# Rows of tokens for the last residual: transposing transfers of 16-bit halves in place of TensorE transposes

## The chip, the cores and the metric

The kernel runs on one core of a Trainium2 chip. The metric is the device time of one execution in microseconds (us); the median of a few runs is compared. A profiled execution gives a trace: TensorE's matmuls (PE) and weight loads (PEld), VectorE (DVE), ScalarE (ACT), GpSimd (POOL), and SyncE (SP), which here only issues DMA transfers.

## The reference

One block of a streaming encoder over 512 tokens of 1024 features, in float32. What matters here:

```
x = x + 0.5 * swiglu(rms_norm(x, ffn1_norm), ffn1_w1, ffn1_w3, ffn1_w2)
h = rms_norm(x, mix_norm); p = h @ w_in
y_a = rwkv7_mixer(...) @ rwkv_proj ; y_b = fox_mixer(...) @ fox_proj
x = x + (gate_a * y_a + gate_b * y_b) @ w_out
x = x + 0.5 * swiglu(rms_norm(x, ffn2_norm), ffn2_w1, ffn2_w3, ffn2_w2)
out = rms_norm(x, final_norm)
swiglu(h, w1, w3, w2) = (silu(h @ w1) * (h @ w3)) @ w2
```

The x after `w_out` is used twice: as the input of the second FFN, and once more as the last residual, to which the FFN's result is added.

## The kernel before, in words

**Layout.** Through the mixer x is kept with features on the partitions: eight tiles `xT[m]` of 128 features x 512 tokens (2 KB a partition), the tiles `xS` by the end. The second FFN's last product gives the other layout, tokens on the partitions. So its residual has to be there by token: a DRAM tensor `osave` of 4 blocks x 128 tokens x 1024 features holds it, and is read back near the end of the kernel.

**Products.** Every float32 product is three matmuls (`mm3`, L173-176): the weights and the data are each split into a high part, rounded to the matmul's format by ACT, and the rest, by DVE (`split_w`, L163-168; tiles `whi`, `wlo`, two of each; the raw weights have three buffers, `raw`). A product of 128 output features over 1024 inputs is 24 matmuls of 128x512.

**The w_out product** (L2061-2069) runs over m = 0 to 7. For each it loads and splits weights, runs 24 matmuls into the bank `pw`, adds half of that to `xT[m]` on DVE, and calls `nrm2.add(m)`: DVE splits the scaled tile into `xh`, `xl`, ACT squares it, and POOL adds the square into `acc` (DVE does the last addition). The engines' order in this loop is the scheduler's, except that the products follow each other.

**The memory around it.** Everything of the mixer that is not needed longer lies in the pool `sp`, closed at the end of the loop by `sctx.close()`. `gslot` names halves of its tiles `G` (512 floats a partition each), free during the w_out product. The second FFN's buffers come from the pool `hp`, which takes over the same memory: the weights' buffers `ca`, `cd`, `cb`, `cc`, `u` and the tiles `seven.lo`, `seven.hi` (`rl`, `rh` in the profile).

**The start of the second FFN.** The raw weights of four products are requested on SP (`load_raw`), then `wide.begin()` requests ten loads of 512 KB into `cd`, `ca`, `cc`, `u`, `cb`, in this order and on SP. From `written(True)` on, the instructions of DVE, ACT and TensorE are issued in the order in which the program writes them (class `Queued`, L87-104; its instructions all have line L102 in the profile). POOL and SP stay with the scheduler. That order is: the first product `pa` (24 matmuls); the sum over squares (`ssum`, two matmuls) and its root (`rstd`, on ACT); then `tokens(m)` for eight m among the matmuls of the product `pb`, with `wide.normal` (DVE, scales the tile of x in place by gain and root) and `wide.weight(0, 0)` (splits the first half of `cd`: ACT's `sraw`, then DVE's) between; then the split of the fourth weights (`whi`, `wlo`) and the products `pa` and `pb` that follow.

`tokens(m)`, the function that the change replaces: four TensorE transposes of 128x128 into a bank `ot`, one ACT copy out of it into `o` (a free half of `seven.hi`, or a temporary), and one POOL store into `osave`.

Of the kernel before, what the change touches and what calls it, by code (L numbers as in the profile page):

```python
# [9 lines left out]
F32 = mybir.dt.float32  # L10
F32R = mybir.dt.float32r
BF16 = mybir.dt.bfloat16
AF = mybir.ActivationFunctionType
ALU = mybir.AluOpType
AX = mybir.AxisListType
# [3 lines left out]
P = 128  # L19
T = 512  # L20
D = 1024
KD = D // P
# [6 lines left out]
NB = T // P  # L29
# [52 lines left out]
def kernel(  # L82
# [6 lines left out]
    nc = tc.nc  # L89
# [16 lines left out]
    pool = nc.gpsimd  # L106
    dve, act, pe = [Queued(e, False) for e in (nc.vector, nc.scalar, nc.tensor)]
# [11 lines left out]
    pf = ctx.enter_context(tc.tile_pool(name="pf", bufs=3, space=PSUM))  # L119
    dp = ctx.enter_context(tc.tile_pool(name="dp", bufs=1, space=DRAM))  # L120

    def bank(name, pool_=None):
        pool_ = pool_ or pm
        return pool_.tile([P, T], F32, tag="b", name=name)

    def tmp(name, shape=(P, T), dt=F32, tag="t", **kw):
        return tp.tile(list(shape), dt, tag=tag, name=name, **kw)


    ident = cp.tile([P, P], F32, name="ident")  # L130
    make_identity(nc, ident)
    identb = cp.tile([P, P], BF16, name="identb")
    dve.tensor_copy(identb[:], ident[:])
# [15 lines left out]
    gmask = cp.tile([P, 2, C], F32, name="gmask")  # L149
    dmask = cp.tile([P, T], BF16, name="dmask")  # L150
    sel = cp.tile([P, 8], F32, name="sel")
# [18 lines left out]
    def load_w(aps, kt, n, eng=None):  # L170
        return split_w(load_raw(aps, kt, n), kt, n, eng)
# [6 lines left out]
    def ln_act(out, in_, **kw):  # L178
        pre = act.preload_act_table_set("natural_log_exp_and_others")
        tc.keep_in_program_order(pre)  # L180
        tc.keep_in_program_order(act.activation(out, in_, AF.Ln, **kw))

# [22 lines left out]
    def on(do, *a):  # L205
        return lambda: do(*a)

    class Plan:
# [4 lines left out]
        def op(s, engine, us, do, *deps, rank=0, takes=(), frees=(), later=0.0, kind="w"):  # L213
            s.ops.append(dict(engine=engine, do=do, deps=deps, takes=takes, frees=frees, done=False))
            return s.ops[-1]
# [20 lines left out]
    xT = [xQ[c // 4][:, c % 4] for c in range(KD)]  # L236
# [9 lines left out]
    class Norm:  # L246
# [7 lines left out]
        def scale(s, c, eng=None, src=None):  # L254
# [3 lines left out]
            if eng is act:  # L258
                high = act.activation(hi[:], src, AF.Copy, scale=g)
            else:  # L260
# [6 lines left out]
        def square(s, c, eng=None, src=None):  # L267
            src = xT[c][:] if src is None else src
            if s.n == 0:
                s.acc = xp.tile([P, T], F32, tag="acc", name="acc", bufs=2)  # L270
                act.activation(s.acc[:], src, AF.Square)
            else:
                sq = tmp("sq")
                act.activation(sq[:], src, AF.Square)
                if s.n < KD - 1:
# [26 lines left out]
    def pc(i):  # L302
        return par[:, i:i + 1]
# [12 lines left out]
    with tc.tile_pool(name="x0", bufs=1) as x0:  # L316
# [27 lines left out]
        def x_hi(c):  # L344
            nrm.hi[c] = pair("h", c)
            from_ = xps[c][:]
            if c % 2:
                qact.activation(nrm.hi[c][:], from_, AF.Copy, scale=pc(PAR_FFN1 + c))
            else:
# [24 lines left out]
        def square(c):  # L374
            if c == 0:
                nrm.acc = xp.tile([P, T], F32, tag="acc", name="acc", bufs=2)
                qact.activation(nrm.acc[:], xT[c][:], AF.Square)
            else:
# [666 lines left out]
    with tc.tile_pool(name="hp", bufs=1) as hp:  # L1045
        hp.tile([P, 96], F32, name="lead")
        wide = Wide(hp, Middle, nrm, ffn1_w1[0], ffn1_w3[0], ffn1_w2[0], xQ,
                    [x[0, b * P:(b + 1) * P, :] for b in range(NB)], C1)
        seven1, rows = wide.seven, []
# [26 lines left out]
        return [(0, W[:, c0:c0 + n])]  # L1076

    nrm2 = Norm(PAR_FFN2)
    with ExitStack() as mx:
        rp = mx.enter_context(tc.tile_pool(name="rp", bufs=1))  # L1080
        sctx = ExitStack()
# [100 lines left out]
        for o, c0, mu in ((spare[2], DA, 4), (spare[3], 0, 0)):  # L1182
            ps = bank("pk", pf)
# [3 lines left out]
        for p in range(NP):  # L1187
            za.append((zslots[2 * p], zslots[2 * p + 1]))
            for i, (w_, x_, par0, o) in enumerate(((uw, lw, PAR_W0, zslots[2 * p]), (ux, lx, PAR_A0, zslots[2 * p + 1]))):
                ps = bank("pz", (pr, pf)[i])  # L1190
# [181 lines left out]
        for t in range(C - 1):  # L1372
            n, m = t + 1, C - 1 - t
# [82 lines left out]
        for b in range(NB):  # L1456
            o = vtp.tile([P, T], F32, name=f"vt{b}", tag=f"vt{b}")
# [12 lines left out]
        rows = [Rows(p, n) for p in range(2) for n in range(2)]  # L1470
# [26 lines left out]
        for q in range(2):  # L1497
            o = (1 - q) * 64
# [11 lines left out]
        for q in range(2):  # L1510
            o = (1 - q) * 64
# [9 lines left out]
        for q in range(2):  # L1521
            pool.memset(Rs[0][half(q), :, q, :], 0.0)
            for i in range(RN):
                o = (1 - q) * 64
# [8 lines left out]
        o = op("ACT", 0.69, b1.log, summed, rank=SCAN, takes=["t"], frees=["pf"])  # L1533
        o = op("ACT", 0.63, b1.root, o, rank=SCAN)
# [110 lines left out]
        for c in range(NC):  # L1645
# [4 lines left out]
            if c % 4 == 3 and c < NC // 2:  # L1650
                o = op("SP", 0.4, on(fetch, nc.sync, c + 5, 4), e, later=4.0)
# [40 lines left out]
        def columns(name, at):  # L1692
            w, split_ = weights(at)

            def some(k):
                if k == 0:
                    w.ps = bank(name)
                mix.cols(w.ps[:], w.hi, w.lo, P, [], [k], k == 0, k == KD - 1)

            for k in range(KD):  # L1700
                fills.append(op("PE", 0.68, on(some, k), split_, *fills[-1:], rank=FILL,
                                takes=["pm"] * (k == 0), frees=["w"] * (k == KD - 1)))
            return w, fills[-1]
# [36 lines left out]
        for m in range(NP + 3, 2 * KD):  # L1740
            g = Held()
            w, o = columns("pgt", COL_GA + m * P)
# [11 lines left out]
            o = op("DVE", 0.61, result, o, rank=NEXT, takes=["gs"], frees=["pm"])  # L1754
            if m + 1 < 2 * KD:
                o = op("ACT", 0.55 if tanhs else 1.84, opened, o, *roots, rank=ROWS)
# [6 lines left out]
        sees, turned, exps, copies, yb = [], ([], []), [], [], []  # L1763
# [143 lines left out]
        o = []  # L1907
        for p in range(NP):
            o = op("ACT", 0.63, on(part_y, p), *outs[p], *sees, *o, rank=FILL)
            o = [op("DVE", 0.69, on(part_l, p), o, rank=FILL)]  # L1910
# [6 lines left out]
        def proj(m, wt, y, w=None):  # L1917
            wh, wl = w or proj_w(m, wt)
            ps = bank("ppj")
            for k in range(NP):  # L1920
                mm3(ps[:], wh[:, k, :], wl[:, k, :], y[k][0], y[k][1], k == 0, k == NP - 1)
            return ps


        def halves(tiles):
            return [t[:, i * 8:(i + 1) * 8].rearrange("p c a t -> p (c a t)") for t in tiles for i in range(2)]

        gslot = halves([g for gg in G for g in gg])
# [11 lines left out]
        ycs, sqs, pgs, pus, parts = [None] * NP, [None] * NP, [None] * NP, [None] * NP, {}  # L1940
# [70 lines left out]
        ps = proj(0, fox_proj, ybs, fws[0])  # L2011
        for m in range(KD):
# [11 lines left out]
            if m + 1 < KD:  # L2024
                ps = proj(m + 1, fox_proj, ybs, fws[m + 1])
# [29 lines left out]
        for m in range(KD):  # L2055
            g = slot[m]
            ps = proj(m, rwkv_proj, ya)
# [4 lines left out]
        for m in range(KD):  # L2062
            wh, wl = load_w([(0, w_out[0][:, m * P:(m + 1) * P])], KD, P)
            ps = bank("pw")
            with tc.issue_after(done.ins) if m else ExitStack():
                for k in range(KD):
                    done = mm3(ps[:], wh[:, k, :], wl[:, k, :], ms[k][0], ms[k][1], k == 0, k == KD - 1)
            dve.scalar_tensor_tensor(xT[m][:], ps[:], 0.5, xT[m][:], op0=ALU.mult, op1=ALU.add)
            nrm2.add(m)
        sctx.close()  # L2070


# [56 lines left out]
                nc.sync.dma_start(out[0, P:2 * P, low], o)  # L2129
                queue.dma_start(out[0, P:2 * P, high], o2)  # L2130

    osave = dp.tile([NB, P, D], F32, name="osave")
    with tc.tile_pool(name="hp", bufs=1) as hp:
        hp.tile([P, 96], F32, name="lead")
        wide = Wide(hp, Last, nrm2, ffn2_w1[0], ffn2_w3[0], ffn2_w2[0], xS, osave)

        def tokens(m):
            ps = bank("ot", pf)
            for b in range(NB):
                pe.transpose(ps[:, b * P:(b + 1) * P], xT[m][:, b * P:(b + 1) * P], ident[:])  # L2140
            o = wide.seven.hi[1][:, m] if m < 4 else tmp("on")[:]
            act.copy(o, ps[:])
            nc.gpsimd.dma_start(osave[:, :, m * P:(m + 1) * P].rearrange("b p c -> p b c"),
                                o.rearrange("p (b c) -> p b c", b=NB))

        raws = [load_raw([(0, w[:, j * P:(j + 1) * P])], KD, P) for j in range(2) for w in wide.w]
        wide.begin()
        ps = [bank("pa"), bank("pb", pr)]
        wide.ssum = bank("ssum", pr)
        written(True)  # L2150
        ws = [split_w(raws[0], KD, P)]
        nrm2.parts()
        ws.append(split_w(raws[1], KD, P))
        act.preload_act_table_set("natural_log_exp_and_others")
        wide.unit(ps[0], ws[0])
        ws.append(split_w(raws[2], KD, P))
        wide.root()
        for m in range(2):
            tokens(m)
        wide.places()  # L2160
        wide.normal(range(2))
        wide.weight(0, 0)
        for m in range(2, KD):
            wide.unit(ps[1], ws[1], (m - 2,))
            tokens(m)
            wide.normal((m,))
        wide.unit(ps[1], ws[1], range(KD - 2, KD))
        pa, pb = bank("pa", pr), bank("pb", pf)
        ws.append(split_w(raws[3], KD, P))
        wide.unit(pa, ws[2])  # L2170
        wide.unit(pb, ws[3])
        wide.weight(0, 1)
        wide.hidden(0, *[t[:] for t in ps])
        wide.weight(1, 0)
        wide.weight(1, 1)
        wide.column(wide.ssum)
        wide.spots()
        wide.blocks(pa, pb, {})
# [24 lines left out]
```

## Time and profile before

| | |
|---|---|
| median of three runs | 1086.06 us (1086.01 to 1086.47) |
| the profiled execution's own time | 1085.94 us |
| its span | 1083.9 us |
| TensorE busy | 1074.8 us (99%) |
| TensorE's clock granted | 0.999 |
| transposes `ot` | 32, started from 752.7 to 760.3 us |
| stores into `osave` | 8 of 256 KB, 6.5 to 10.6 us to landing (median 8.4) |
| reads of `osave` | from 839.8 us on |

Times within the trace count from the start of the span. A line of the trace gives the start, the duration, the engine, the line of the kernel, the operation, what it writes and reads, and in brackets how long its engine was idle before and what ended that. "SPq" and "POOLq" are the issuing queues. In the chain of waits each step is the work that released the next one.

### The profile page before, as it was taken

To read this page: it belongs to the slowest core of one execution; us is meant where nothing else is said; L and a number is where in the kernel's file an instruction comes from. 1 tells how busy PE (TensorE), PEld (TensorE's weight loads), DVE (VectorE), ACT (ScalarE), POOL (GpSimd) and SP (SyncE) were. 2 spreads that over 40 slices of the span, in tenths; PEclk is the share of its full clock that TensorE was granted. 3 is DMA by queue.
4 is the path that set the end of the run, shared out by engine and by line. 5 is a ranking of instruction groups with operands and counts; after the bars stand their busy time and mean duration, and the time that the engine had idled before them with its cause. 6 is when DMAs were issued, how large, how long until landed. Compare 5 with 4: busy or idle time off the path is not lost.

```text
span 1083.9 us, 16868 instructions
## 1 busy us (share of the span) xinstructions
PE 1074.8 (99%) x6378; PEld 883.9 (82%) x6378; DVE 833.2 (77%) x1155; ACT 673.7 (62%) x1055; POOL 212.5 (20%) x259
## 2 busy tenths in 40 slices
PE   9999999999999999999999999999999999999997
PEld 7888888888887887888788787888888888888886
DVE  7998576789865699888787777867597666699874
ACT  6765556576555766435889877524576555576554
POOL 1221220134203212402000130123311212114210
PEclk9999999999999999999999999999999999999999
DMA  7989988879945443444212354636967979869972
GB/s 219 255 171 235 209 170 201 189 146 188 232 127 168 114 112 106 124 136 114 82 46 82 99 154 128 195 116 202 245 156 176 205 202 185 191 151 203 236 188 78
DMA packets 142095, 177.13 MB, mean 163 GB/s; under 512 B 12094, under 2 KB 78206, under 8 KB 142014
## 3 DMA queue, kind: packets, MB, share of 16 engines
q0 software_dynamic: 33392, 70.14, 33.9%
q1 hardware_dynamic: 107886, 104.48, 31.5%
q10 hardware_dynamic: 736, 1.45, 0.3%
q8 instruction: 50, 0.82, 0.3%
q14 instruction: 31, 0.25, 0.1%
HBM read 163.51 MB, written 12.52 MB: 162 GB/s over the span
## 4 chain that ended last, share of the span: by engine, by line
PE 97%; DVE 1%; ACT 1%; issue 0%; DVEq 0%; ACTq 0%
PE P L102 40%; PE P L176 6%; PE P L174 6%; PE P L175 6%; PE pgt L102 5%; PE l L102 3%; PE spot L102 3%; PE pq L102 3%; PE ppj L102 2%; PE pk L176 2%; PE pk L174 2%; PE pk L175 2%; PE pb L102 2%; PE pa L102 2%; PE pw L175 1%; PE pw L174 1%
## 5 line engine op out<-in xcount | busy, mean ns | idle before, releaser
L102 PE MATMUL P<-sraw,q 128*128 128x512 f32 x344 | 91.3, 389 | 0.0
L102 PEld LDWEIGHTS P<-sraw,q 128*128 128x128 f32 x344 | 64.6, 188 | 13.4
L102 PE MATMUL P<-swhi,q 128*128 128x512 f32 x224 | 71.4, 390 | 0.0
L166 ACT CAST whi<-raw 128x1024 fp32r<-128x1024 f32 (+2 forms) x42 | 40.4, 962 | 48.8 <-issue 19.3
L102 PE MATMUL P<-sraw,wxh 128*128 128x512 f32 x200 | 68.4, 394 | 0.0
L102 PE MATMUL P<-swhi,wxh 128*128 128x512 f32 x144 | 56.9, 395 | 0.0
L102 PE MATMUL P<-swhi,wxl 128*128 128x512 f32 x144 | 56.1, 390 | 0.0
L102 PE MATMUL P<-swlo,wxh 128*128 128x512 f32 x144 | 56.1, 389 | 0.0
L167 DVE TENSOR_TENSOR wlo<-raw,whi 128x1024 fp32r<-128x1024 f32 (+2 forms) x43 | 48.4, 1127 | 9.6 <-ACT whi L166 8.5
L692 POOL DMA_DIRECT2D cb<-in_ffn_w_dram x20 | 24.1, 1203 | 150.8 <-DVE cd L102 85.1
L102 PE MATMUL P<-sraw,wxl 128*128 128x512 f32 x136 | 53.0, 390 | 0.0
L692 POOL DMA_DIRECT2D cd<-in_ffn_w_dram x24 | 29.5, 1230 | 102.5 <-DVE swlo L102 37.5
L102 PEld LDWEIGHTS P<-swhi,q 128*128 128x128 f32 x224 | 42.0, 188 | 8.7
L102 PE MATMUL P<-swlo,q 128*128 128x512 f32 x112 | 43.6, 389 | 0.0
L102 PEld LDWEIGHTS P<-sraw,wxh 128*128 128x128 f32 x200 | 37.2, 188 | 7.3
L102 ACT COPY RD<-spot 32x128 f32<-32x128 f32 (+2 forms) x128 | 39.9, 311 | 5.3 <-PE spot L102 2.3
L102 ACT CAST sraw<-cd 128x1024 fp32r<-128x1024 f32 x30 | 31.5, 1051 | 14.9 <-PE P L102 11.5
L102 DVE TENSOR_TENSOR swlo<-ca,swhi 128x1024 fp32r<-128x1024 f32 x24 | 29.2, 1221 | 14.0 <-ACT swhi L102 14.0
L102 DVE TENSOR_TENSOR u<-P,u 128x512 f32<-128x512 f32 x52 | 34.1, 683 | 5.8 <-ACT u L102 5.8
L176 PE MATMUL pk<-xh,wlo 128*128 128x512 f32 x96 | 37.5, 393 | 1.0 <-DVE wlo L167 1.0
L174 PE MATMUL pk<-xh,whi 128*128 128x512 f32 x96 | 38.0, 396 | 0.4 <-DVE u L1227 0.4
L102 DVE TENSOR_TENSOR swlo<-cc,swhi 128x1024 fp32r<-128x1024 f32 x20 | 24.5, 1224 | 18.0 <-ACT swhi L102 17.6
(623 smaller groups left out, 3418.9 us busy)
## 6 DMA issues: line engine op xcount, KB each, us to landing
raw<-in_w_in_dram SPq DMA_DIRECT2D x40, 512.0 KB
cc<-in_ffn_w_dram SPq DMA_DIRECT2D x36, 512.0 KB
cb<-in_ffn_w_dram POOLq DMA_DIRECT2D x36, 512.0 KB, 6.0
cb<-in_ffn_w_dram SPq DMA_DIRECT2D x32, 512.0 KB
cd<-in_ffn_w_dram POOLq DMA_DIRECT2D x32, 512.0 KB, 7.8
ca<-in_ffn_w_dram POOLq DMA_DIRECT2D x32, 512.0 KB, 7.4
ca<-in_ffn_w_dram SPq DMA_DIRECT2D x20, 512.0 KB
cd<-in_ffn_w_dram SPq DMA_DIRECT2D x18, 512.0 KB
```

What stands on the lines that cost most here:

```text
L102: q.last = do(*a, **kw)
L166: (hi_eng or act).copy(hi[:], raw[:])
L167: (eng or dve).tensor_tensor(lo[:], raw[:], hi[:].bitcast(F32), op=ALU.subtract)
L174: pe.matmul(ps, whi, xhi, start=first, stop=False, skip_group_check=onto)
L175: pe.matmul(ps, whi, xlo, start=False, stop=False, skip_group_check=onto)
L176: return pe.matmul(ps, wlo, xhi, start=False, stop=last, skip_group_check=onto)
L692: nc.gpsimd.dma_start(to, s.block(b, n, h), accum_op=ALU.add)
```

## The change

`tokens` no longer uses TensorE. It regards each float32 of `xT[m]` as two 16-bit halves. ACT copies the low halves of all 512 tokens, then the high halves, into a tile `parts` (1024 elements of 16 bits a partition); one transfer on SP with `transpose=True` turns the eight blocks of 128x128 16-bit elements of it into `turned`; POOL copies the low and the high halves back to their places, two copies of 512 elements with a stride of two, into `rows`; and POOL stores `rows` into `osave`, as before. Bits are only moved; nothing is rounded.

For m = 0 to 5 (`AHEAD` = 6) it is called in the w_out product, behind `nrm2.add(m)`, with three halves of the `G` tiles in `sp` as `parts`, `turned` and `rows`: one set for even m, another for odd m. For m = 6 and 7 it is called where the first two were, behind `wide.root()`, with parts of `seven.hi` and `seven.lo`. The calls among the matmuls of `pb` are gone. `osave` is allocated earlier.

```diff
+    osave = dp.tile([NB, P, D], F32, name="osave")
+    AHEAD = KD - 2
+
+    def tokens(m, parts, turned, rows):
+        parts, turned, to = [t.bitcast(U16) for t in (parts, turned, rows)]
+        for s in range(2):
+            act.copy(parts[:, s * T:(s + 1) * T], xT[m][:].bitcast(U16).rearrange("p (t s) -> p t s", s=2)[:, :, s])
+        nc.sync.dma_start(turned.rearrange("p (b c) -> p b c", c=P), parts, transpose=True)
+        for s in range(2):
+            pool.tensor_copy(to.rearrange("p (t s) -> p t s", s=2)[:, :, s], turned[:, s * T:(s + 1) * T])
+        nc.gpsimd.dma_start(osave[:, :, m * P:(m + 1) * P].rearrange("b p c -> p b c"),
+                            rows.rearrange("p (b c) -> p b c", b=NB))
...
             nrm2.add(m)
+            if m < AHEAD:
+                tokens(m, *gslot[m % 2:6:2])
         sctx.close()
...
-        def tokens(m):
-            ps = bank("ot", pf)
-            for b in range(NB):
-                pe.transpose(ps[:, b * P:(b + 1) * P], xT[m][:, b * P:(b + 1) * P], ident[:])
-            o = wide.seven.hi[1][:, m] if m < 4 else tmp("on")[:]
-            act.copy(o, ps[:])
-            nc.gpsimd.dma_start(osave[:, :, m * P:(m + 1) * P].rearrange("b p c -> p b c"),
-                                o.rearrange("p (b c) -> p b c", b=NB))
...
         wide.root()
-        for m in range(2):
-            tokens(m)
+        for m in range(AHEAD, KD):
+            tokens(m, *[(wide.seven.hi, wide.seven.lo)[m % 2][0][:, i] for i in range(1, 4)])
         wide.places()
         wide.normal(range(2))
         wide.weight(0, 0)
         for m in range(2, KD):
             wide.unit(ps[1], ws[1], (m - 2,))
-            tokens(m)
             wide.normal((m,))
```

More of the change, by code (lines that the diff above doesn't have):

```diff
@@ L12 @@
 BF16 = mybir.dt.bfloat16
+U16 = mybir.dt.uint16
 AF = mybir.ActivationFunctionType
@@ L2130, in finished @@
                 queue.dma_start(out[0, P:2 * P, high], o2)
-    osave = dp.tile([NB, P, D], F32, name="osave")
     with tc.tile_pool(name="hp", bufs=1) as hp:
```

## The prediction

> **What bounds the kernel now.** I read the totals first, then the chain of waits, then the stretch in which the tokens are made.
>
> ```profile
> span 1083.9 us, 16868 instructions
> PE 1074.8 (99%) x6378; PEld 883.9 (82%) x6378; DVE 833.2 (77%) x1155; ACT 673.7 (62%) x1055; POOL 212.5 (20%) x259
> PE 97%; DVE 1%; ACT 1%; issue 0%; DVEq 0%; ACTq 0%
> ```
>
> TensorE is 97% of the chain that ends last, so time taken from it is time of the kernel wherever nothing else comes late instead. The chain in order of time, around the change (start, us, what):
>
> ```profile
> 746.99 5.44 PE pa L102 x24
> 752.43 0.46 PE ssum L102 x2
> 752.89 0.87 PE ot L102 x8
> 753.76 0.69 PE pb L102 x3
> ...
> 760.13 0.44 PE ot L102 x4
> 760.57 1.39 PE pb L102 x6
> 761.96 5.46 PE pa L102 x24
> ```
>
> The eight groups of transposes (`ot`) sit among the 24 matmuls of the first `pb` product. There is no gap: TensorE waits for nothing here.
>
> **Removed: 32 transposes.** From 752.89 to 761.96 are 9.07 us, in which 24 matmuls of `pb` stand too; 24 such matmuls without transposes take 5.44 us (row 746.99). So the transposes cost 9.07 - 5.44 = **3.63 us**, all of it on the chain. That is 0.33% of the time and the most that the change can bring. Also removed are eight ACT copies out of PSUM and eight POOL stores in this stretch. Neither engine is on the chain there.
>
> **Moved into the w_out product: tokens 0 to 5.** Each now needs two ACT copies, a transposing transfer on SP, two POOL copies and a POOL store. What DVE, ACT and POOL do there around m = 5 and 6 (start, us, what), with the group of DVE's operations into `xl` (duration min/median/max, ns) and the busy time of PE, PEld, DVE, ACT and POOL, the clock, the DMA share and the GB/s of one stretch:
>
> ```profile
> 736.14 0.69 DVE L2068 SCALAR_TENSOR_TENSOR xS<-pw,xS 128x512 f32<-128x512 f32 x1 [1.39 <-PE pw L176]
> 742.71 1.22 DVE L102 TENSOR_TENSOR wlo<-raw,whi 128x1024 fp32r<-128x1024 f32 x1
> 735.96 1.05 ACT L166 CAST whi<-raw 128x1024 fp32r<-128x1024 f32 x1 [3.86 <-issue]
> 736.93 0.64 ACT L274 ACTIVATE sq<-xS 128x512 f32<-128x512 f32 x1
> 743.15 1.94 POOL L276 TENSOR_TENSOR acc<-acc,sq 128x512 f32<-128x512 f32 x1 [3.50 <-ACT sq L274]
> L262 DVE SCALAR_TENSOR_TENSOR xl<-xS,par,xh x8: 748/1786/1789, 711.2 to 748.3; 128x512 fp32r<-128x512 f32 x8
> 742.00:747.00 5.00, 5.00 (x23) 4.14 (x23) 3.60 (x4) 1.00 (x2) 1.94 (x1) 1.00 0.34 99
> ```
>
> A product takes 5.44 us. ACT idles 3.86 us of it (brackets of the cast), POOL 3.50; the DMA engines are 0.34 busy from 742 to 747. Two copies of 128x512 on ACT at the 0.64 us of the square are 1.3 us: hidden in 3.86, and nothing on TensorE is behind them but the next cast of `whi`, which has a whole product to spare. POOL's copies can block DVE: `xl` takes 1.79 us beside POOL's sum and 0.75 us alone. The split that must be in time is `wlo`; at 742.71 + 1.22 = 743.93 it is 3.4 us ahead of the product of 746.99 that reads it (with its third matmul), so one or two POOL copies in its way cost nothing.
>
> POOL's copy of 128x512 16-bit elements is not in the trace. The nearest rows bound it, and these bound the transfer and the store:
>
> ```profile
> L2143 POOL DMA_DIRECT2D osave<-rh x4 | 3.0, 766 | 10.9 <-ACT rh L102 10.9
> L1469 POOL MEMSET klc<- 128x512 f32 x2 | 1.0, 531 | 0.0
> L1527 POOL COPY RD<-ident 64x256 f32<-64x256 f32 x6 | 4.2, 721 | 0.2
> L276 POOL TENSOR_TENSOR acc<-acc,sq 128x512 f32<-128x512 f32 x6 | 11.8, 1960 | 47.2 <-ACT sq L274 47.2
> DMA to landing us min/median/max: 2.3/3.7/7.1
> DMA to landing us min/median/max: 6.5/8.4/10.6
> ```
>
> The copy costs 0.53 to 1.96 us; I take 1.0, nearer the copy and the fill than the two-input sum. The fifth row is the 256 KB stores and loads of the gates (`gsave`) at light traffic, the last the stores of `osave` now, which run where the DMA engines are full. No transposing transfer is in the trace: for its 256 KB I take bounds of 2.3 and 10.6 us, and 3.7 within them, since it starts at 0.34 busy engines, like the gates. In POOL's period that makes 1.95 + 2 x 1.0 + 0.77 of store issue = 4.7 of 5.44 us. It fits; at 1.96 a copy it would not (6.6).
>
> [...]
>
> **The wait that can come in.** The last FFN's buffers (`hp`) take the memory of the pool `sp` that the mixer gives back at the end of the w_out product. SP's and the last stage's rows now:
>
> ```profile
> 747.06 0.88 SPq L689 DMA_DIRECT2D cd<-in_ffn_w_dram  x2
> SPq L689 <- PE pw L176: 2.5, 1, 2.5
> 751.23 0.58 SPq L689 DMA_DIRECT2D cb<-in_ffn_w_dram  x1
> SPq L689 <- DMA cd<-in_ffn_w_dram: 0.5, 1, 0.5
> 702.92 0.39 PE L176 MATMUL ppj<-ya,wlo 128*128 128x512 f32 x1
> ```
>
> By the sizes of the tiles, the first half of `cd` lies over BK2 and BK3 only, whose last reader (`ya`) is done at 703.3; yet its load waited until the last `pw` matmul at 747. So the wait is for everything in `sp`, and the nine loads behind it on SP wait too. In the changed kernel the three slots of each token lie in `sp`, so the first load waits also until the store of token 5 has landed. Call that time R. Worked out: x of m = 5 is final at 736.83; the square ends at 737.57; two copies 738.8; transfer 3.7: 742.5; POOL's copies 2.0 and perhaps the sum of m = 6 (1.95) between: 746.5; store issue 0.77 and landing 3.7: **R = 751**, 749 without the sum between. R is 2 to 4 us later than today's 747.06. What that does is in the last stage (ACT, then DVE, then the DMA after it):
>
> ```profile
> 754.22 0.63 ACT L102 ACTIVATE rstd<-rstd 128x512 f32<-128x512 f32 x1
> 754.76 1.06 ACT L102 COPY rh<-ot 128x512 f32<-128x512 f32 x2
> 755.70 1.06 ACT L102 CAST sraw<-cd 128x1024 fp32r<-128x1024 f32 x1
> 756.80 1.23 DVE L102 TENSOR_TENSOR sraw<-cd,sraw 128x1024 fp32r<-128x1024 f32 x1 [0.50 <-ACT sraw L102]
> 757.94 4.06 DVE L102 SCALAR_TENSOR_TENSOR xS<-xS,par,rstd 128x512 f32<-128x512 f32 x6
> 762.85 1.23 DVE L102 TENSOR_TENSOR wlo<-raw,whi 128x1024 fp32r<-128x1024 f32 x1 [0.85 <-ACT whi L102]
> 755.00:760.00 5.00, 5.00 (x32) 4.08 (x31) 4.50 (x7) 4.34 (x8) 4.01 (x6) 1.00 1.05 386
> 759.02 1.25 POOL L692 DMA_DIRECT2D cd<-in_ffn_w_dram  x1
> DMA to landing us min/median/max: 6.2/7.4/10.2
> 786.79 1.06 ACT L102 CAST sraw<-cd 128x1024 fp32r<-128x1024 f32 x1 [0.18 <-ACT q L102]
> 839.81 0.81 SPq L689 DMA_DIRECT2D xS<-osave  x2
> ```
>
> Orders of ACT and DVE are written out here. The new kernel puts four copies (tokens 6 and 7) ahead of the cast `sraw<-cd`, where two stood: at 0.53 (half of row 754.76) to 0.64 us it starts at 756.9 to 757.3, not 755.70. DVE follows: its split 1.1 after the cast's start, then 1.2, six scalings 4.06 and `wlo` 1.2 make 7.5 from the cast's start, so `wlo` ends at 764.4 to 764.8. Its reader is the third matmul of the second `pb`. Without transposes `pa` starts at 752.89 + 5.44 = 758.3, `pb` at 763.8, that matmul 0.45 later, at 764.2. So TensorE stalls there for **0.2 to 0.6 us**, I take 0.4: today's slack of 3.8 us (`wlo` done at 764.08, read at 767.42 + 0.45) is used up by the gain.
>
> R enters by `cd`: its first half landed by 751.23 (the `cb` load that follows doesn't wait for it, the next waits for the second half), so within 4.2 us of 747.06. At R + 4.2 <= 756.9, that is R up to **752.7**, it costs nothing; later, each us costs a us, and at 752.7 + 3.2 = 755.9 the gain is gone. My R of 749 to 751 is below.
>
> **Tokens 6 and 7** transfer behind the ten loads on SP (DMA engines full, 1.05, in the stretch from 755 to 760); POOL's copies and stores follow at about 765. Behind them on POOL may stand the adding load into `cd`, now issued at 759.02, 10.2 us to landing at most (the row after it, for `cd`), read at 786.79. Issued at 768 instead it lands by 778, and it is read at 783.6 when TensorE is 3.2 us ahead. The rows in `osave` are read at 839.81. Both are hidden; with that cover gone each us of delay would cost a us.
>
> **Sum.** -3.63 + 0.4 = -3.2 us, against the profiled execution's own 1085.94 (its span of 1083.9 and 2.0 around it): 1082.7; that run is 0.12 below the median of 1086.06, so I predict **1082.8**.
>
> **Rivals.**
>
> *Slower: the transfers are slow and take turns, and `sp` comes back late.* Place: the first `cd` load on SP. If a transposing transfer holds its queue for D us, six from 711.6 on (x of m = 0 is five products of 5.44 before 736.83, at 709.6; square and copies 2.0) end at 711.6 + 6D, and R is 6.4 later (copies, issue, landing). It decides from 711.6 + 6D + 6.4 = 755.9, D = 6.3. At D = 7.5, R = 763, `wlo` ends at 763 + 4.2 + 7.5 = 774.7, 10.5 us late: 1086.1 - 3.6 + 10.5 = **1093**; at D = 10.6 in the same way 1112. POOL, in order, would hold the sum for `ssum` behind the same transfer. For it: eight blocks of 16-bit elements, and the 10.6 us row. Against: the 3.7 us median and idle DMA engines. [...]
>
> *No difference: part of the gain is lost on DVE or in R.* If tokens 6 and 7 land before `wlo`, two POOL copies of 1.0 stand in the way of DVE's scalings (two SBUF inputs, as `xl`): 2.0 + 0.4 lost, **1084.9**. R at 755 gives about the same. Against: the transfers stand behind ten loads.
>
> *The gain is whole* (1082.4) if the four copies take the shorter time; I count it with the forecast.
>
> **How the numbers follow.** Forecast (1082.2 to 1083.9): 0.55. Part lost (1083.9 to 1088.2): 0.22. Slower: 0.23, spread from 1088 to beyond 1100. A measurement of this kernel tells about 0.2%, 2.2 us, from no change, so faster means below 1083.9. Below 1082.2 nothing is left to gain. The range 1082.0 to 1089.0 leaves out most of the slower case, some 0.2; the forecast's own is 1082.2 to 1083.9.
>
> **What would show it.** Right: no `ot` matmuls; the first `pb` product takes 5.44 us in the chain; the first `cd` load at 749 to 752; a small wait of TensorE for `wlo` near 764. Wrong: transposing transfers over 6 us to landing, the first `cd` load after 756 with TensorE idle behind `wlo` or `ssum`, or a wait for `raw` in the w_out product.

## The result and the profile after

The changed kernel takes **1082.44 us** (median of 6 runs, 1082.29 to 1083.12), the kernel before 1086.03 beside it (1085.81 to 1086.47): ratio 0.9967, 95% interval 0.9955 to 0.9979. That is 3.6 us or 0.33% less; 1082.8 was forecast, with 1082.2 to 1083.9 as its own range.

The totals of the changed kernel, and the shares of its chain of waits:

```profile
span 1081.3 us, 16859 instructions
PE 1072.1 (99%) x6346; PEld 881.2 (81%) x6346; DVE 829.7 (77%) x1155; ACT 677.4 (63%) x1063; POOL 223.9 (21%) x275
PE 96%; DVE 2%; ACT 1%; issue 1%; DMA 0%; ACTq 0%; DVEq 0%
```

TensorE has 32 matmuls fewer and is 2.7 us less busy; ACT and POOL have taken on 3.7 and 11.4 us. This execution is the slowest of its six (1083.12), and it is late before the change's place: the first product of the last FFN (`pa`) starts at 747.65, not 746.99. It is late already at the first `pw` matmul of the w_out product, which starts at 703.81, not 703.15. From there to the first matmul of `pa` are 43.67 us, 43.68 in the kernel before: the work that moved into the w_out product costs TensorE nothing there. So the traces are compared from the row of `pa` on. Up to the start of the first matmul into the banks `P`, which follows the second `pb` product, the kernel before took 773.08 - 746.99 = 26.09 us, the changed one 770.51 - 747.65 = 22.86: **3.23 us less**. Its chain there (start, us, what), and what TensorE's weight loads waited for:

```profile
747.65 4.25 PE pa L103 x19
...
763.82 1.14 DVE wlo L103
...
765.00 5.29 PE pb L103 x22
...
770.51 9.55 PE P L103 x42
```

```profile
PEld pb L103 <- DVE wlo L103: 0.5, 1, 0.5
```

The `ot` matmuls are gone. Followed back, the chain leaves TensorE at 765.0: of the second `pb` product's 24 matmuls two are done, and the weight load of the third waits 0.5 us for the fourth `wlo`. That is the stall the prediction had put there.

The moved work: the tiles `G` between 705 and 800 (duration min/median/max in ns, first and last start; the landing times are those of the six stores into `osave`), then rows of SP, POOL, ACT and DVE in order of time within each. Lines stand one lower than in the kernel before.

```profile
L1086 ACT COPY G<-xS x12: 602/610/618, 710.9 to 738.6; 128x512 uint16<-128x512 uint16 x12
L1089 POOL COPY G<-G x12: 758/899/1215, 717.7 to 746.8; 128x512 uint16<-128x512 uint16 x12
L1087 SPq DMA_TRANSPOSE G<-G x6: 1237/1862/2511, 712.4 to 739.7; - x6
DMA to landing us min/median/max: 2.7/2.9/4.0
```

```profile
734.45 1.72 SPq L1087 DMA_TRANSPOSE G<-G  x1
751.01 0.88 SPq L690 DMA_DIRECT2D cd<-in_ffn_w_dram  x2
757.62 8.51 SPq L1087 DMA_TRANSPOSE rh<-rh  x1
...
739.03 1.88 POOL L1089 COPY G<-G 128x512 uint16<-128x512 uint16 x2 [2.12 <-DMA G<-G]
741.61 1.31 POOL L277 TENSOR_TENSOR acc<-acc,sq 128x512 f32<-128x512 f32 x1
742.85 0.91 POOL L1090 DMA_DIRECT2D osave<-G  x1
743.81 1.93 POOL L277 TENSOR_TENSOR acc<-acc,sq 128x512 f32<-128x512 f32 x1
745.70 1.89 POOL L1089 COPY G<-G 128x512 uint16<-128x512 uint16 x2
747.88 0.77 POOL L1090 DMA_DIRECT2D osave<-G  x1 [0.30 <-POOL G L1089]
760.40 1.22 POOL L693 DMA_DIRECT2D cd<-in_ffn_w_dram  x1 [11.74 <-DMA ca<-in_ffn_w_dram]
775.05 2.84 POOL L1089 COPY rl<-rl 128x512 uint16<-128x512 uint16 x2 [0.24 <-DMA rl<-rl]
...
756.44 1.14 ACT L103 COPY rl<-xS 128x512 uint16<-128x512 uint16 x2
757.48 1.04 ACT L103 CAST sraw<-cd 128x1024 fp32r<-128x1024 f32 x1
763.73 1.22 DVE L103 TENSOR_TENSOR wlo<-raw,whi 128x1024 fp32r<-128x1024 f32 x1
```

The reader is to see three things. The first `cd` load stands at 751.01, behind the store of token 5 (747.88), where it stood at 747.06. The cast `sraw<-cd` at 757.48 follows the four copies of tokens 6 and 7 without a gap, so it doesn't wait for `cd`. And the transfer of token 4, issued at 734.45, ends POOL's wait at 739.03, 4.6 us later; for tokens 0, 2 and 3 it is 5.3, 5.5 and 4.7 us.

### The profile page after: what moved, and what is told of

The parts are those of the page before. It is cut to its first block, busy times and chain, and to the rows that moved or that the text cites. A ratio compares the mean times of both kernels' runs of the same rounds, so it can differ in the third digit from the quotient of the medians.

```text
span 1081.3 us, 16859 instructions
## 1 busy us (share of the span) xinstructions
PE 1072.1 (99%) x6346; PEld 881.2 (81%) x6346; DVE 829.7 (77%) x1155; ACT 677.4 (63%) x1063; POOL 223.9 (21%) x275
## 4 chain that ended last, share of the span: by engine, by line
PE 96%; DVE 2%; ACT 1%; issue 1%; DMA 0%; ACTq 0%; DVEq 0%
PE P L103 40%; PE P L176 6%; PE P L175 6%; PE P L177 6%; PE pgt L103 5%; PE l L103 3%; PE spot L103 3%; PE pq L103 3%; PE ppj L103 2%; PE pk L177 2%; PE pk L175 2%; PE pk L176 2%; PE pw L176 1%; PE pw L177 1%; PE pw L175 1%; PE f L103 1%
## 5 line engine op out<-in xcount | busy, mean ns | idle before, releaser
L552 POOL DMA_DIRECT2D ca<-in_ffn_w_dram x16 | 19.3, 1205 | 95.8 <-DVE swlo L103 66.5
```

Of the source, the lines that this page charges most:

```text
L552: nc.gpsimd.dma_start(s.sum[g], src, accum_op=ALU.add)
```

## The experiments

The theory: the gain is the 32 transposes; the price is the stall for `wlo`, which comes from the order on ACT and DVE; the return of the pool `sp` (R, the first `cd` load) costs nothing as long as it is early enough. The rivals: the transfers are near a limit of their own (they take turns, or fill the DMA engines), or R already costs something.

The executions differ by up to 1 us in where `pa` starts. The table takes that out by the time from `pa`'s start in the chain of waits to the end of the span. (With seven tokens and with doubled transfers the chain doesn't pass through `pa`; there its start is the first matmul's, 747.55 and 747.14, and the 0.17 us by which the chain has it later elsewhere.)

| kernel | us, median (lowest to highest) | ratio to before, interval | `pa` to end |
|---|---|---|---|
| before | 1086.03 (1085.81 to 1086.47) | | 336.9 |
| after | 1082.44 (1082.29 to 1083.12) | 0.9967 (0.9955 to 0.9979) | 333.7 |
| e1_no_transpose | 1082.04 (1081.92 to 1082.41) | 0.9964 (0.9952 to 0.9977) | 333.3 |
| e2_split_first | 1082.03 (1081.87 to 1082.71) | 0.9964 (0.9952 to 0.9977) | 333.3 |
| e3_ahead7 | 1088.62 (1087.1 to 1089.29) | 1.0021 (1.0012 to 1.0031) | 339.9 |
| e4_twice | 1089.6 (1088.28 to 1090.91) | 1.0031 (1.0016 to 1.0045) | 341.0 |
| e5_plain | 1082.43 (1082.34 to 1082.81) | 0.9966 (0.9954 to 0.9978) | 333.6 |
| e6_first_ahead7 | 1083.05 (1082.52 to 1083.76) | 0.9968 (0.9957 to 0.9979) | 333.7 |
| e7_first_ahead8 | 1085.59 (1084.69 to 1087.31) | 0.9996 (0.9988 to 1.0005) | 337.2 |
| e8_twice_apart | 1082.81 (1082.59 to 1083.61) | 0.9971 (0.9959 to 0.9983) | 333.9 |

### The transposes alone

The kernel before without the 32 transposes: the residual's rows are copied as they are, not turned, so that part of the output is another.

```diff
-            ps = bank("ot", pf)
-            for b in range(NB):
-                pe.transpose(ps[:, b * P:(b + 1) * P], xT[m][:, b * P:(b + 1) * P], ident[:])
...
-            act.copy(o, ps[:])
+            act.copy(o, xT[m][:])
```

> The kernel before with its 32 transposes left out: ACT copies x as it stands (features on the partitions), so what is added as the last residual is not turned and the output is another one; the eight ACT copies, the eight stores among the ten loads and the order of everything else stay. Theory (the gain is TensorE's 3.63 us and nothing else): 1086.0 - 3.6 = 1082.4 us, no wait of TensorE near 764, since two copies instead of four stand ahead of the cast of cd. Rival (the gain comes from taking ACT's and POOL's work out of this stretch): no change, 1086.0. Rival (the transposes cost less than their place in the chain shows): between the two.

Measured: 1082.04. Its chain of waits stays on TensorE:

```profile
747.16 5.44 PE pa L102 x24
...
769.64 10.46 PE P L102 x46
```

From `pa` to `P` it takes 22.48 us, 3.61 less than before; by the table 3.6 to the end. So the transposes are worth what the chain of before said, 3.63, and nothing later gives any of it back. The changed kernel stays 22.86 - 22.48 = 0.38 us short of it: that is its stall.

### The stall: the split ahead of six scalings

In the changed kernel, the matmuls of the first `pb` product stay in their order, but the last split is written out ahead of six of DVE's eight scalings.

```diff
-        for m in range(2, KD):
-            wide.unit(ps[1], ws[1], (m - 2,))
-            wide.normal((m,))
-        wide.unit(ps[1], ws[1], range(KD - 2, KD))
+        wide.unit(ps[1], ws[1])
         pa, pb = bank("pa", pr), bank("pb", pf)
         ws.append(split_w(raws[3], KD, P))
+        wide.normal(range(2, KD))
```

> The changed kernel with the split of the fourth weights (whi, wlo) issued ahead of the six scalings of x, in place of behind them. Theory (the wait of 0.5 us before the second pb is DVE's order): wlo ends at about 761, the wait is gone, 1082.4 - 0.5 = 1081.9 us, and nothing is late behind it, since the scaled x is first read at 775. Rival (cd comes late because sp comes back late): wlo still waits behind the split of cd, the wait stays, 1082.4.

Measured: 1082.03, the best of the kernels run. The end of the same stretch in its chain, and SP's load:

```profile
747.10 5.44 PE pa L103 x24
...
763.92 5.44 PE pb L103 x24
...
769.59 10.46 PE P L103 x46
```

```profile
750.46 0.88 SPq L690 DMA_DIRECT2D cd<-in_ffn_w_dram  x2
```

The wait for `wlo` is gone, and the stretch takes 22.49 us, as with no token work on TensorE at all. R is still 750.5, so R costs nothing here. The medians of this kernel and the changed one are 0.4 us apart, as the stretches are (0.37), but their runs overlap; the claim rests on the traces.

### R later: one more token in the product

```diff
-    AHEAD = KD - 2
+    AHEAD = KD - 1
```

> The changed kernel with token 6, too, made in the w_out product (AHEAD = 7). Theory (the first load of the last FFN waits for everything in sp, the store of the last such token with it): the first cd load is issued one product of 5.44 us later, at 756.4 in place of 751.0; cd 4.2 later, wlo 7.5 after that ends at 768.1 against 764.9 that TensorE needs: 3.3 us of wait in place of 0.5, 1082.4 + 2.8 = 1085.2 us. Rival (the loads need only their own memory): the first cd load stays near 748 to 751, two ACT copies fewer stand ahead of the cast, 1081.9.

Measured: 1088.62, slower than before. The chain, then TensorE's rows around the wait, then the stretches of half a microsecond in which its clock changes (busy time of PE, PEld, DVE, ACT, POOL with instructions; clock; DMA share; GB/s):

```profile
752.35 4.64 DMA osave<-G
...
757.33 4.00 DMA cd<-in_ffn_w_dram
...
763.69 4.06 DVE xS L103 x6
768.93 7.61 PE pb L103 x22
```

```profile
764.60 0.39 PE L103 MATMUL pb<-xl,whi 128*128 128x512 f32 x1
768.93 0.79 PE L103 MATMUL pb<-xh,wlo 128*128 128x512 f32 x1 [3.94 <-DVE wlo L103]
```

```profile
767.00:767.50 0.50, 0.00 (x0) 0.00 (x0) 0.50 (x2) 0.00 (x0) 0.05 (x1) 0.53 1.07 393
773.50:774.00 0.50, 0.50 (x3) 0.40 (x2) 0.05 (x1) 0.00 (x0) 0.15 (x1) 0.64 1.10 262
```

The chain goes just the way the prediction had drawn for a late R: store of the last token in `sp`, `cd` load, cast, split, six scalings, `wlo` (from 767.75), TensorE. R is 757.33, behind a store that takes 4.6 us to land. The third `pb` matmul comes at 768.93 instead of 764.83 (0.23 behind the one before it): 4.1 us. But the loss is larger. The same 22 matmuls take 7.61 us where they took 5.29 (0.43 us from start to start at first, then 0.23), because the granted clock is 0.5 from 767.0 to 773.9. That is another 2.3; together 6.4, and from the table 339.9 - 333.3 = 6.6.

### R later, but with the split ahead of what needs it

Both edits, with the split ahead of all eight scalings; in the next kernel the eighth token in the product too (`AHEAD = KD`).

```diff
-    AHEAD = KD - 2
+    AHEAD = KD - 1
...
-        wide.normal(range(2))
-        wide.weight(0, 0)
-        for m in range(2, KD):
-            wide.unit(ps[1], ws[1], (m - 2,))
-            wide.normal((m,))
-        wide.unit(ps[1], ws[1], range(KD - 2, KD))
+        wide.unit(ps[1], ws[1])
         pa, pb = bank("pa", pr), bank("pb", pf)
         ws.append(split_w(raws[3], KD, P))
+        wide.normal(range(2))
+        wide.weight(0, 0)
+        wide.normal(range(2, KD))
```

> The changed kernel with token 6 in the w_out product, as in e3_ahead7, and with the split of the fourth weights issued ahead of the split of cd and of the scalings, on ACT and DVE. Theory (sp coming back late costs time only because the fourth split stands behind the split of cd): the first cd load stays near 757, but wlo ends near 761, TensorE waits nowhere: 1081.9 us. Rival (the late loads themselves cost): TensorE waits for cd, cc or u, 1083 us or more.

Measured with seven tokens: 1083.05, where 1081.9 was expected. From its SP, POOL and TensorE's weight loads:

```profile
757.46 0.89 SPq L690 DMA_DIRECT2D cd<-in_ffn_w_dram  x2
787.19 3.03 POOL L1089 COPY rl<-rl 128x512 uint16<-128x512 uint16 x2 [12.97 <-DMA rl<-rl]
82.65 0.30 PEld L103 LDWEIGHTS P<-swhi,q 128*128 128x128 f32 x2 [0.47 <-DVE q L103]
820.08 0.30 PEld L103 LDWEIGHTS P<-swhi,q 128*128 128x128 f32 x2 [0.50 <-DVE q L103]
```

R is as late as in the kernel with 1088.62, and TensorE doesn't wait for `wlo`, nor for `cd`, `cc` or `u`. So it isn't the late pool that costs 6 us, but what DVE has ahead of `wlo` behind it. What is left (333.7 against 333.3) goes with one wait of 0.50 us of TensorE's weight loads for DVE's `q`, at 820.08. That a late R causes it is not shown: the same wait, 0.47 us, stands at 82.65 in the first FFN of this execution, which no edit touches. POOL, which waited 13 us for token 7's transfer, issued its adding loads of `cb` later than in the changed kernel (from 791.31, not 788.17); whether that plays a part was not tried.

> The same with all eight tokens in the w_out product (AHEAD = 8). Theory: the first cd load comes another 5.4 us later, near 763, its first half lands at 767, the cast of it ends at 768, 1.5 us before the first P matmul reads it (769.4): no wait, 1081.9 us; with cc and u landing about 772 and 775 against casts at 773 and 779. Rival (the loads are now too late): TensorE waits for the split of cd, some 2 us, 1084 us.

Measured with eight: 1085.59, no gain left; the expectation that nothing would wait was wrong. From the rows of SP, DVE and TensorE, and stretches of half a microsecond as above:

```profile
760.69 0.89 SPq L690 DMA_DIRECT2D cd<-in_ffn_w_dram  x2
772.65 0.73 PE L103 MATMUL P<-sraw,xh 128*128 128x512 f32 x2 [1.96 <-DVE sa L103]
```

```profile
774.00:774.50 0.50, 0.50 (x3) 0.43 (x2) 0.50 (x2) 0.11 (x1) 0.00 (x0) 0.62 1.10 262
777.50:778.00 0.50, 0.50 (x3) 0.38 (x2) 0.36 (x1) 0.14 (x1) 0.00 (x0) 0.96 1.11 254
```

R is 760.69, and now the scalings are late for the next reader: DVE does them, then `extra`, then at 771.91 `sa`, which empties the bank `pa` for `P`'s matmuls. TensorE waits 1.96 us there: the matmul starts at 772.65 instead of 770.52 (0.23 behind the one before it), 2.1 us late. Then the granted clock is 0.5 from 774.1 to 777.5: the eight matmuls from 774.15 to 777.56 take 3.41 us, where the eight from 778.48 to 780.30 take 1.82, which loses 1.6. The sum is 3.7; the table has 337.2 - 333.3 = 3.9. So with the split first, R may be 757.5 at almost no cost, but not 760.7.

### Twice the transposing transfers

First with the second transfer in the same chain, each block turned into `rows` and then into `turned`:

```diff
-        nc.sync.dma_start(turned.rearrange("p (b c) -> p b c", c=P), parts, transpose=True)
+        for to_ in (to, turned):
+            nc.sync.dma_start(to_.rearrange("p (b c) -> p b c", c=P), parts, transpose=True)
```

> The changed kernel with each transposing transfer issued twice (the first into the tile rows, which POOL then overwrites). Theory (a transposing transfer keeps the DMA engines busy: their share rose from 0.27 to 0.99 from 720 to 730, so about 3.2 us a transfer): 8.6 us of transfers in a product of 5.44, so the six run 3.2 us later each time, the first cd load is issued at about 770, and wlo is 17 us late: 1099 us, or more where raw weights come late in the w_out product. Rival (the share shows transfers that wait, not work): the second transfer adds one latency of some 4 us, the first cd load is at 755, 1084.2.

Measured: 1089.6, with R at 757.64. Two rows of its chain:

```profile
746.98 2.79 DMA osave<-G
749.79 3.03 DMA G<-G
```

This run decided nothing about the transfers. The added one writes `rows`, so it must wait for the store of an earlier token out of it, as the chain shows: store, transfer, POOL's copies, store, one after another. It made R late by a wait that the experiment itself had put in. The next one writes where nobody reads or stores:

```diff
+        if m < AHEAD:
+            nc.sync.dma_start(gslot[6 + m % 2].bitcast(U16).rearrange("p (b c) -> p b c", c=P), parts, transpose=True)
```

> The changed kernel with a second transposing transfer for each of tokens 0 to 5, ahead of the first and into a tile of its own that nothing reads, so that it waits for nothing but the ACT copies. Theory A (a transfer keeps the DMA engines busy for some 3.2 us): 8.6 us of transfers in a product of 5.44, six transfers later by 3.2 us each, first cd load near 770, over 1095 us. Theory B (a transfer is mostly issue on SP, 1.9 us, and latency): the needed one follows 1.9 us behind, the first cd load at 753, 1082.4 to 1083.0 us.

Measured: 1082.81. Its first `cd` load, and the busiest ten microseconds, before those of the changed kernel:

```profile
751.41 0.88 SPq L690 DMA_DIRECT2D cd<-in_ffn_w_dram  x2
720.00:730.00 10.00, 10.00 (x46) 8.29 (x45) 8.07 (x8) 4.85 (x8) 6.46 (x5) 1.00 1.24 187
```

```profile
720.00:730.00 10.00, 10.00 (x45) 8.28 (x45) 5.95 (x8) 5.22 (x8) 5.81 (x8) 1.00 0.99 190
```

Twelve transfers instead of six, two in each 5.44 us, bring R to 4.4 us behind `pa`'s start of 746.97, where it stands 3.4 behind in the changed kernel, and cost 0.2 us by the table; the only wait of TensorE's weight loads in the product is 0.3 us for DVE's `ml`, as in the changed kernel. Two such transfers in 5.44 us also show that one doesn't hold its queue for the 6.3 us of the slower rival.

### Plain transfers

Plain copies in place of the transposing ones: the residual's rows aren't turned, and that part of the output is another.

```diff
-        nc.sync.dma_start(turned.rearrange("p (b c) -> p b c", c=P), parts, transpose=True)
+        nc.sync.dma_start(turned.rearrange("p (b c) -> p b c", c=P), parts.rearrange("p (b c) -> p b c", c=P))
```

> The changed kernel with plain copies of the same 256 KB in place of the transposing transfers (the blocks are not turned, so the residual and with it the output are others). Theory (the 4.6 us to landing and the DMA share of 0.99 from 720 to 730 belong to the transposing form): SP issues a copy in 0.4 us in place of 1.2 to 2.5, it lands after 2.3 to 3.7 us, the share falls to about 0.5, the first cd load comes some 1.5 us earlier than 751.0; the time stays 1082.4 us, since R of 751 cost nothing. Rival (any 256 KB within SBUF costs this much): issue, landing and share as in the changed kernel.

Measured: 1082.43, the changed kernel's time. From the tile `G`, SP and POOL, and the same ten microseconds:

```profile
L1087 SPq DMA_DIRECT2D G<-G x6: 471/531/589, 711.7 to 739.0; - x6
738.99 0.53 SPq L1087 DMA_DIRECT2D G<-G  x1
751.05 0.88 SPq L690 DMA_DIRECT2D cd<-in_ffn_w_dram  x2
743.45 2.22 POOL L1089 COPY G<-G 128x512 uint16<-128x512 uint16 x2 [1.96 <-DMA G<-G]
745.60 1.28 POOL L277 TENSOR_TENSOR acc<-acc,sq 128x512 f32<-128x512 f32 x1
746.83 1.72 POOL L1090 DMA_DIRECT2D osave<-G  x2
720.00:730.00 10.00, 10.00 (x46) 8.29 (x45) 5.77 (x8) 4.86 (x8) 5.84 (x8) 1.00 0.62 187
```

A plain transfer of the same 256 KB, issued at 738.99, ends POOL's wait at 743.45: 4.5 us. For tokens 0, 2 and 3 it is 4.5, 5.4 and 4.3 us, where the transposing transfers took 5.3, 5.5 and 4.7: turning lengthens it by 0.1 to 0.8 us. What else it costs is SP's time to issue it (1.86 us in the median, not 0.53) and DMA share (0.99, not 0.62). R is 751.05, not earlier, as had been expected (4.1 us behind `pa`'s start, and 3.4 in the changed kernel). The scheduler has put POOL's work in another order here: POOL waits for the last transfer, copies, and then does one more sum and two stores. So this run doesn't show what R would be with plain transfers in the changed kernel's order. It does show that the kernel isn't faster without the turning.

## Why the prediction was right, and where its steps were off

**Removed, 3.63 us: right.** The first experiment measured 3.61 in the stretch and 3.6 to the end. With the stall taken off, the sum gave 3.2, and the stretch of the changed kernel gave 3.23. The medians are 3.6 apart. No row shows where the other 0.4 come from; executions of one kernel differ by more than that (1082.29 to 1083.12), so it is the stretch that confirms the sum to a tenth, and not the medians.

**The stall for `wlo`, 0.4 us: right, in place, size and cause.** TensorE's weight load waits 0.5 us, the stretch loses 0.37 to 0.38, and moving one split removes it. The working nearly holds too: taking off the 0.66 us by which this execution is late, the cast starts at 756.82 (756.9 to 757.3 was said) and `wlo` ends at 764.29 (764.4 to 764.8), both 0.1 us ahead of what was said.

**R = 751: right as a time, in part by luck.** Measured 751.01, or 750.35 less the 0.66. POOL's sum for m = 6 does stand ahead of token 5's copies, as assumed, but the sum went through token 5's transfer, and no wait for it shows. POOL works on from 739.03 with token 4's copies, two stores and two sums, and starts token 5's copies at 745.70 without a wait. By the 4.6 to 5.5 us of the others, that transfer, issued at 739.65, had landed by then (an estimate: 744.2 to 745.2). So it was 0.9 to 1.8 us slower than the 3.7 assumed, without moving R. The copies end at 746.9 in the time of the kernel before (746.5 was said). From the start of the store's issue to R are 3.13 us, where the sum had 4.47: it added 0.77 of issue to a time to landing that already counts from the issue. The terms are off both ways and nearly cancel. The `cd` load took 4.0 us in the kernel with seven tokens, where 4.2 was assumed. SP's issue of 1.24 to 2.51 us and the DMA share of 0.99, which the sum lacked, cost nothing that can be seen: without either, plain transfers gain nothing.

**The wait is for the whole pool: confirmed.** R moved with the last token stored from `sp`: 751.0 for six, 757.3 and 757.5 for seven, 760.7 for eight.

**"Later, each us costs a us": this step was wrong.** It did not touch the forecast, since R stayed below 752.7, but it mis-sized the rivals. A late R costs its wait and then TensorE's clock: in the kernel with seven tokens 4.1 us of wait, then 2.3 more; with eight and the split first 2.1, then 1.6. The price of these two waits is 1.6 and 1.8 times their length; the changed kernel's wait of 0.5 us has no such addition (clock 1.00 from 763 to 780).

**Tokens 6 and 7 hidden: right, in another order.** POOL takes the adding load of `cd` first, at 760.40, and token 7's copies only at 775.05, not the reverse. They could not stand in DVE's way ahead of `wlo`, as the second rival had it (in the product DVE's `xl` took 1.20 us beside token 3's copies, and 0.75 with POOL idle). Token 6's transfer took SP 8.51 us to issue alone, over the 6 us that the prediction named as a sign of being wrong; but that was behind the ten loads, where nothing on the chain waited for it.

**The slow transfers: this rival falls.** In the w_out product a transfer lands in 4.6 to 5.5 us (3.0 in the row at 749.79 of the doubled transfers), under the 6.3 from which it decided, and twice as many cost 0.2 us. The eight blocks that spoke for it lengthen the transfer by 0.1 to 0.8 us only: a plain one lands in 4.3 to 5.4 us.

## What to carry to other kernels

Where TensorE is nearly the whole chain, small work is worth taking off it even when the substitute is long and roundabout (here some 11 us a token: two ACT copies 1.2, the transfer 4.6 to 5.5, two POOL copies 1.8, the store 2.9), if its result is needed late. Then look at two things: what the borrowed memory keeps from being given back, and which instruction of the written-out orders loses its slack when TensorE runs ahead; here one split, moved ahead of six scalings, gave the last 0.4 us. A stall of TensorE should be counted with the clock behind it: here those of 2.1 and 4.1 us cost 1.6 and 2.3 us more, and the one of 0.5 us nothing more.

## What was not expected of the hardware

**Behind three waits TensorE's clock was at half, for 3.42 us or twice that.** The waits are of 1.96 us (eight tokens), 3.94 us (seven tokens) and 4.71 us (the doubled transfers in one chain). From the clocks of the half-microsecond rows, with full clock for the one part of the slice and 0.5 for the other, the clock falls at 774.12 and is back at 777.54 in the kernel with eight tokens: 3.42 us. In the one with seven it falls at 767.03 and is back at 773.86: 6.83, twice that. With the doubled transfers it falls at 768.29 and is back at 775.11: 6.82. In the last 3.42 us ahead of the fall TensorE had idled 1.95 us with eight tokens, 2.0 with seven and all 3.42 with the doubled transfers; the changed kernel's wait of 0.5 us brought no fall (1.00 in each such row from 763 to 780). What a wait between 0.5 and 1.96 us does, and what sets the lengths, these runs don't show. In the 3.42 us behind the fall TensorE idled 1.9 us with seven tokens and 1.0 us with the doubled transfers, and in both the 3.42 us after that were at half clock too; with eight tokens it idled nowhere in them, and the clock was back after the 3.42.

**A transposing transfer took its issuer longer.** In the changed kernel's w_out product SP took 1.24 to 2.51 us to issue 256 KB, where a plain one took 0.47 to 0.59. Behind the ten loads, at a DMA share of 1.05 (from 755 to 760), the issue lasted 8.51 us (row 757.62; 0.62 for the plain transfer in that place), and the next transfer on that queue was issued only at 766.24.
